# RWKV-7 mixer: one layout for both directions, halves and heads, and a recurrence without GpSimd arithmetic

## The chip, the cores and the metric

The kernel runs on one core of a Trainium2 chip. The metric is the device time of one execution in microseconds (us), the median of the runs. The engines are named as in the profile: PE is TensorE's matmul stream and PEld its loads of stationary operands, DVE is VectorE, ACT is ScalarE, POOL is GpSimd, SP is SyncE, which here only issues DMA transfers. TensorE runs at one of two clock levels, 1.2 and 2.4 GHz; the profile shows the share of the full one that was granted (PEclk).

## The reference, cut to what matters

The model is a trunk of two layers. A layer mixes tokens by three groups of heads in parallel and ends in a mixture of experts. The change is in the first group, the bidirectional RWKV-7 recurrence, and in the input columns of the two attention groups beside it. The recurrence, over 256 context and 1024 latent tokens, with 4 heads of 64 and two directions:

```
def _rwkv7_step(state, inp):                 # state: direction, head, v, k
    r, w, k, v, kk, a = inp
    sk = einsum('dbhvk,dbhk->dbhv', state, kk)
    state = state * w[..., None, :] - sk[..., :, None] * (kk * a)[..., None, :] \
            + v[..., :, None] * k[..., None, :]
    return state, einsum('dbhvk,dbhk->dbhv', state, r)
```

Here w is the decay, a the learning rate of a token, kk the normalised key, and k depends on the direction through a. The columns of the attentions are `h @ w_in`, with a rotation of q and k of the sliding-window group.

## The kernel before

The recurrence is computed in chunks of 64 tokens. A step `st` of ten handles, for both directions d, a segment of 128 tokens, that is two chunks c; heads come as two pairs hp with a head e of each pair in one half of the 128 partitions (`hom[e]`). So there are 8 units (d, hp, c) in each half.

Function `rwkv` has three parts for each step.

1. `front(st)` loads r, k, kk and the low-rank inputs, computes decays and their sums along a chunk (`cum`, by a scan, line 746) and forms scaled operands: `kd`, the direction's key (line 765, POOL), `L1` with kk and r times the decays (lines 776 and 777, DVE for e = 0 and POOL for e = 1), `bk` with the counterparts (line 784 on DVE, 785 on POOL), and `bw` (line 788, POOL). It is called for the next step ahead of the work of the present one.
2. Per step, products of `bk` and `L1` inside a chunk (line 824, tile `pa`, two banks, one for each e) are masked into `L1`, `Ly` and `low` (lines 829 to 833, 841). `low` is a lower triangle of 64 x 64 for each unit. Its inverse is made in `inv16`: the 16 x 16 blocks go through memory (`lan`) into a layout with a block on a partition, are inverted by 28 small DVE operations (lines 955 and 956) and come back through memory (`inv`); then products at line 853 (`pe`, `pzt`, `pz`), 864, 873 and 875 join the blocks.
3. Two scan steps s, one for each chunk: the old state X times `L1` (line 904, `px`), a copy (906), a product with the inverse (912), the negated values into X (913 on ACT, 914 on DVE), products for the new state and the output (924, 926), and the new state (930) from the decayed old one (`xw`, line 897, POOL). Outputs `ys` are added in eight DVE operations (935) and stored once a step by SP. New values are put in X by `new_pvu` (line 713, ACT).

Beside it, `in_BC` computes the attention columns. A column tile is 24 matmuls into one PSUM bank (lines 528 to 530, or 539 to 541), then ACT scales the result (1065), for the rotated tiles TensorE, DVE and POOL rotate it (1068 to 1072), and `part` splits it in a high and a low float16 half (1042 on ACT, 1043 on POOL). It is a generator; `more()` advances it at three places of a step.

The order of each engine's instructions is not that of the code. A scheduler takes the next instruction by a timeline that it computes when the kernel is built; the engines then run their lists in order. Rotating buffers (two PSUM banks for parts 1 and 2, two for the scan steps, one for the inverse, three for the columns) decide how far it can run ahead.

The line that splits a product's operand between engines, and the one that gives a tile two banks:

```
eng = v if e == 0 else g                                                     # before line 776
pas = [ps.tile([P, 512], F32, tag=tag, name="pa") for _ in range(2)]         # before line 824
```

## Time and profile before

| | us |
|---|---|
| median of 3 runs (lowest to highest) | 3548.71 (3547.73 to 3562.64) |
| the profiled execution | 3544.36 |
| its span | 3541.6 |
| PE busy | 2930.6 (83%) |
| DVE busy | 2285.5 (65%) |
| ACT busy | 1544.1 (44%) |
| POOL busy | 1007.7 (28%) |

Busy shares are means over stages of different kinds: the input columns of the recurrence, the recurrence with the attention columns beside it, the attentions, the output projection, the experts, for each layer. In the slices of the page below, of 88.5 us each, the recurrence fills the slices 3 to 8 of layer 0 and 23 to 28 of layer 1. DVE's digits reach 8 there, TensorE's are 8 and 9 for the most part.

### The profile page before, as it was taken

Reading aid. Unit: us, or ns where it says so; the run is one execution under the profiler, and the core shown is the slowest. Engines: PE = TensorE matmul, PEld = TensorE weight load, DVE = VectorE, ACT = ScalarE, POOL = GpSimd, SP = SyncE. Lnnn points to the kernel's source line nnn. Section 1 sums busy time; section 2 is a strip of 40 time slices with the busy share of each in tenths; the row PEclk is TensorE's granted clock in tenths of the full one; section 3 lists DMA queues with packets and bytes.
Section 4 is the critical chain, followed back from the end, with each engine's and each line's share of the span. In section 5 each row is a group of like instructions: output and inputs, shape, how many; then the busy total and the mean of one; then the engine's idle time right before and its main releaser. Section 6 shows DMA issues by size and latency. Waiting matters only on the chain. (4 is left out here: it accounts for less than half of the span.)

```text
span 3541.6 us, 71217 instructions
## 1 busy us (share of the span) xinstructions
PE 2930.6 (83%) x28620; PEld 1833.0 (52%) x28620; DVE 2285.5 (65%) x4614; ACT 1544.1 (44%) x2769; POOL 1007.7 (28%) x998
## 2 busy tenths in 40 slices
PE   7998889989998788888737998898889866778864
PEld 4656567666755444443325565666666443334431
DVE  4356877368769454557678677783776845554775
ACT  4342444345643154456544434443565314343651
POOL 1122453134424211111165225331433321101113
PEclk9998889999999899999858988899899978888987
DMA  9764343282355789999862542433732769899995
GB/s 375 297 194 111 80 104 89 70 237 71 113 176 199 278 315 384 385 379 367 334 227 78 158 106 77 105 103 95 200 107 73 258 235 363 338 393 364 349 347 198
DMA packets 425468, 773.11 MB, mean 218 GB/s; under 512 B 211152, under 2 KB 340848, under 8 KB 394160
## 3 DMA queue, kind: packets, MB, share of 16 engines
q1 hardware_dynamic: 388048, 697.84, 56.7%
q0 software_dynamic: 36368, 68.07, 5.7%
q8 instruction: 227, 3.72, 0.4%
q10 hardware_dynamic: 720, 2.62, 0.3%
q14 instruction: 105, 0.86, 0.1%
HBM read 653.31 MB, written 114.97 MB: 217 GB/s over the span
## 5 line engine op out<-in xcount | busy, mean ns | idle before, releaser
L1664 PE MATMUL pgate<-wgp,hT 128*32 128x256 f16 (+2 forms) x1704 | 353.1, 376 | 101.8 <-ACT wgp L1613 60.8
L1664 PEld LDWEIGHTS <-hT 128*32 128x32 f16 (+2 forms) x3408 | 206.7, 108 | 334.0 <-issue 172.7
L529 PE MATMUL acc<-hL,wH 128*128 128x256 f16 (+2 forms) x1040 | 346.4, 334 | 13.4 <-POOL hL L486 13.4
L528 PE MATMUL acc<-hH,wH 128*128 128x256 f16 (+2 forms) x1040 | 345.6, 335 | 7.6 <-DVE hH L485 6.6
L530 PE MATMUL acc<-hH,wL 128*128 128x256 f16 (+2 forms) x1040 | 345.4, 333 | 0.0
L1704 PE MATMUL pd<-wdp,gT 128*32 128x256 f16 (+2 forms) x1704 | 221.1, 369 | 37.6 <-DVE gT L1691 21.6
L1195 POOL TENSOR_SCALAR s<-s,rd 128x640 f32<-128x640 f32 (+2 forms) x216 | 171.6, 794 | 222.3 <-DVE rd L1191 97.4
L1622 POOL DMA_INDIRECT xg<-hmoe,map x69 | 87.7, 1271 | 508.4 <-PE ptx L1628 454.5
L1664 PE MATMUL pgate<-wup,hT 128*32 128x256 f16 (+1 forms) x1224 | 196.9, 347 | 19.8 <-DVE wup L1614 12.7
L1614 DVE SCALAR_TENSOR_TENSOR wgp<-wg,wgp 128x2048 f16<-128x2048 f32 x74 | 166.4, 2287 | 63.2 <-ACT wgp L1613 63.1
L1614 DVE SCALAR_TENSOR_TENSOR wdp<-wd,wdp 128x2048 f16<-128x2048 f32 x74 | 166.5, 2287 | 46.9 <-ACT wdp L1613 46.9
L1184 ACT ACTIVATE s<-s,nm 128x640 f32<-128x640 f32 (+2 forms) x216 | 164.4, 763 | 66.1 <-DVE nm L1181 48.6
L1614 DVE SCALAR_TENSOR_TENSOR wup<-wu,wup 128x2048 f16<-128x2048 f32 x74 | 166.3, 2286 | 30.0 <-ACT wup L1613 27.7
L1208 PE MATMUL po<-pt,vt 128*64 128x128 f32 x1920 | 166.9, 288 | 20.2 <-DVE pt L1199 11.7
L1293 PE MATMUL acco<-wo,o 128*128 128x512 f16 x756 | 177.2, 388 | 0.0
L1704 PEld LDWEIGHTS <-gT 128*32 128x32 f16 (+2 forms) x1704 | 97.0, 108 | 147.4 <-DVE gT L1691 30.0
L1613 ACT ACTIVATE wdp<-wd 128x2048 f16<-128x2048 f32 x74 | 137.2, 1903 | 51.0 <-DMA wd<-w_down 44.1
L1717 POOL DMA_DIRECT2D ys<-y x66 | 51.7, 784 | 378.5 <-DVE y L1711 206.9
L1613 ACT ACTIVATE wup<-wu 128x2048 f16<-128x2048 f32 x74 | 137.3, 1903 | 48.7 <-DMA wu<-w_up 48.7
L1613 ACT ACTIVATE wgp<-wg 128x2048 f16<-128x2048 f32 x74 | 137.4, 1902 | 46.0 <-DMA wg<-w_gate 42.7
L1165 PE MATMUL pss<-k,qs 128*128 128x256 f16 (+1 forms) x552 | 127.5, 269 | 31.9 <-DVE mx L1178 18.4
L1672 ACT ACTIVATE sg<-pgate 64x512 f32<-64x512 f32 (+2 forms) x86 | 42.8, 498 | 251.9 <-PE pgate L1664 251.9
(420 smaller groups left out, 7424.2 us busy)
## 6 DMA issues: line engine op xcount, KB each, us to landing
wu<-w_up SPq DMA_DIRECT2D x64, 2048.0 KB
wd<-w_down SPq DMA_DIRECT2D x64, 2048.0 KB
wg<-w_gate SPq DMA_DIRECT2D x64, 2048.0 KB
wmod<-w_mod SPq DMA_DIRECT2D x48, 1024.0 KB
w<-w_in SPq DMA_DIRECT2D x41, 512.0 KB
ld<-ys SPq DMA_DIRECT2D x40, 384.0 KB
z<-inv SPq DMA_DIRECT2D x80, 128.0 KB
ys<-y POOLq DMA_DIRECT2D x20, 512.0 KB
```

Source lines behind the costliest of these rows:

```text
L528: self.nc.tensor.matmul(ov, H[:, k, :], hh, start=k == 0, stop=False)
L529: self.nc.tensor.matmul(ov, H[:, k, :], hl, start=False, stop=False)
L530: self.nc.tensor.matmul(ov, Lo[:, k, :], hh, start=False, stop=k == KD - 1)
L1165: te.matmul(pss[:, o:o + n], qs[:, e, Q], k1[:, e, k0:k0 + n], start=True, stop=False)
L1184: a.activation(s2[:, e, :nk], s2[:, e, :nk], AF.Exp, bias=nm[:, e:e + 1], scale=1.0 / SS, accum_out=den[:, e:e + 1])
L1195: g.tensor_scalar(s2[:, e, :nk], s2[:, e, :nk], rd[:, e:e + 1], SC_Q, OP.mult, OP.mult)
L1208: te.matmul(po[64 * e:64 * e + 64, 0:P], vt[:, kb, 64 * e:64 * e + 64], pt[:, e, x * P:x * P + P], start=x == 0, stop=x == len(kbs) - 1)
L1293: te.matmul(acc, o[:, zo, k] if k < KD - 1 else self.og_last[:, zo, tok], wo[:, zw, k, c], start=k == 0 and y == 0, stop=k == KD - 1 and y ...
L1613: nc.scalar.mul(t[:, 0, c], w[:, c], SC_W)
L1614: nc.vector.scalar_tensor_tensor(t[:, 1, c], w[:, c], SC_W, t[:, 0, c], OP.mult, OP.subtract)
L1664: te.matmul(p[off + i * m:off + i * m + m, :n], part(hT, zh)[:, k, o:o + m], part(w, zw)[:, k, i * n:i * n + n], start=k == 0 and y == 0, ...
L1704: te.matmul(t, part(gT, zh)[:, k, :m], part(wd, zw)[:, k, i * n:i * n + n], start=k == 0 and y == 0, stop=k == 3 and y == len(parts) - 1)
```

## The change

The tiles `L1`, `L2`, `Ly`, `X`, `xy` get another order of their axes, so that one operation covers both directions or both halves, where two or four did. The product at line 824 is split: the part that goes to the other half (`pk`, one bank for both halves, line 825 of the new file) and, as products of 64 columns, those for `Ly` (`pr`, 839) and `low` (`pf`, 842, now for both directions). The products of the inverse at 853 (now 862) take only the 32 of 64 columns that are not known to be zero or unchanged; their result E lies in a tile of its own, E4, that is cleared once a layer. POOL's operations in `front`, `xw`, the rotation and the low halves go to DVE, and `bw` goes to ACT in eight pieces. Tiles that are not rotated are no longer copied before they are split: ACT writes the high half and DVE the low one, both from the accumulator. `ys` is stored for each direction and scan step, the values are loaded in three transfers in place of two.

```diff
+        E4 = rp.tile([P, 8, 64], F32, name=f"E4{l}")
+        g.memset(E4, 0.0)
...
-            for d, seg in enumerate((FSEG[st], BSEG[st])):
-                nc.sync.dma_start(vt[st][:, d], self.vst[:, 2 * seg:2 * seg + 2])
+            nc.sync.dma_start(vt[st][:, :, 0], self.vst[:, 2 * FSEG[st]:2 * FSEG[st] + 2])
+            for s in range(2):
+                nc.sync.dma_start(vt[st][:, s, 1], self.vst[:, 2 * BSEG[st] + 1 - s])
...
-            for d in range(2):
-                for e in range(2):
-                    o = hom[1 - e]
-                    a.copy(t[o, d, :, :, e, :], vt[st][o, d, s if d == 0 else 1 - s].unsqueeze(1).to_broadcast([64, 2, 2, 64]))
+            for e in range(2):
+                o = hom[1 - e]
+                a.copy(t[o, :, :, :, e, :].rearrange("p x d h v -> p x (d h) v"),
+                       vt[st][o, s].rearrange("p d h v -> p (d h) v").unsqueeze(1).to_broadcast([64, 2, 4, 64]))
...
-                for hp in range(2):
-                    v.tensor_tensor_scan(cum[:, d, hp], k2("scan"), th[:, d, hp], 0.0, OP.mult, OP.add)
+                v.tensor_tensor_scan(cum[:, d].rearrange("p h t -> p (h t)"), k2("scan"), th[:, d].rearrange("p h t -> p (h t)"), 0.0, OP.mult, OP.add)
...
-            g.tensor_tensor(kd, ta, k_, OP.mult)
+            v.tensor_tensor(kd, ta, k_, OP.mult)
...
-            for d in range(2):
-                for e in range(2):
-                    eng = v if e == 0 else g
-                    eng.tensor_tensor(L1v[hom[e], d, :, e, e], chv(kk_)[hom[e], d], chv(ex)[hom[e], d], OP.mult)
-                    eng.tensor_tensor(L1v[hom[e], d, :, e, 1 - e], chv(r_)[hom[e], d], chv(cum)[hom[e], d], OP.mult)
...
-                g.tensor_tensor(bku[o, :, 1 - e], units(kd)[o], units(wv)[o], OP.mult)
+                v.tensor_tensor(bku[o, :, 1 - e], units(kd)[o], units(wv)[o], OP.mult)
+            L1p = L1.rearrange("p d h c e s t -> p d (h c) e s t")
+            for e in range(2):
+                o = hom[e]
+                for i, (x, y) in enumerate(((kk_, ex), (r_, cum))):
+                    v.tensor_tensor(L1p[o, :, :, e, i], pieces(x)[o], pieces(y)[o], OP.mult)
...
-            g.tensor_tensor(bw.rearrange("p d h c s t -> p (d h c) (s t)"), bk.rearrange("p d h c s t -> p (d h c) (s t)"),
-                            wt.rearrange("p d h c -> p (d h c)").unsqueeze(2).to_broadcast([P, 8, 128]), OP.mult)
+            wtu = wt.rearrange("p d h c -> p (d h c)")
+            for i, (x, y) in enumerate(((bw[:, d, h, c], bk[:, d, h, c]) for d in range(2) for h in range(2) for c in range(2))):
+                a.activation(x, y, AF.Copy, scale=wtu[:, i:i + 1])
...
-                pas = [ps.tile([P, 512], F32, tag=tag, name="pa") for _ in range(2)]
+                pk = ps.tile([P, 4, 128], F32, tag=tag, name="pk")
...
-                            te.matmul(pas[e][:, i * 128:i * 128 + 128], bk[hom[e], d, hp, c].rearrange("p s t -> p (s t)"),
-                                      L1[hom[e], d, c, hp, e].rearrange("p s t -> p (s t)"), start=True, stop=True)
+                            te.matmul(pk[hom[1 - e], 2 * hp + c], bk[hom[e], d, hp, c, 1 - e, :],
+                                      L1[hom[e], d, hp, c, e].rearrange("p s t -> p (s t)"), start=True, stop=True)
...
+                            te.matmul(pr[hom[e], i], b_, r1, start=True, stop=True)
+
+                            x, y = (K_, b_) if d == 0 else (b_, K_)
+                            te.matmul(pf[hom[e], i], x, y, start=True, stop=True)
+            v.tensor_tensor(Ly.rearrange("p d h c t -> p d (h c) t"), pr.rearrange("p (d u) t -> p d u t", d=2),
+                            k2("mR").rearrange("p (d t) -> p d t", d=2).unsqueeze(2).to_broadcast([P, 2, 4, 64]), OP.mult)
+            v.tensor_tensor(low.rearrange("p d h c t -> p (d h c) t"), pf, k2("mLow").unsqueeze(1).to_broadcast([P, 8, 64]), OP.mult)
...
-            E = rp.tile([P, 8, 64], F32, tag="E", name="E", bufs=1)
-            v.tensor_tensor(E, mm8("pe4", lowu, zt16), k2("mE4").unsqueeze(1).to_broadcast([P, 8, 64]), OP.mult)
-            v.tensor_tensor(zt16, zt16, mm8("pzt", z16, E), OP.subtract)
-            v.tensor_tensor(z16, z16, mm8("pz", E, z16), OP.subtract)
+            lo16, up16 = halves(z16)[:, :, :, 0], halves(zt16)[:, :, :, 1]
+            Eh = halves(E4)[:, :, :, 1]
+            v.tensor_tensor(Eh, mm8("pe4", lowu, up16), k2("mE4").rearrange("p (g t) -> p g t", t=16).unsqueeze(1).to_broadcast([P, 8, 2, 16]), OP.mult)
+            pzt = mm8("pzt", z16, Eh)
+            v.tensor_tensor(up16, up16, pzt, OP.subtract)
+            v.tensor_tensor(lo16, lo16, mm8("pz", E4, lo16), OP.subtract)
...
-                        g.tensor_tensor(xw[hom[e]], X[hom[e], :, 0, :, e, :], w, OP.mult)
+                        v.tensor_tensor(xw[hom[e]], X[hom[e], 0, :, :, e, :], w, OP.mult)
...
-                for e in range(2):
-                    o = hom[1 - e]
-                    for d in range(2):
-                        c = s if d == 0 else 1 - s
-                        v.tensor_tensor(ys[o, d, c], pm[o, 1, d], xy[o, d, :, e, :], OP.add)
+                ys = rp.tile([P, 2, 2, 64], F32, tag="ys", name="ys", bufs=2)
+                v.tensor_tensor(ys, pm[:, 1], xy[:, 1], OP.add)
+                for d in range(2):
+                    nc.sync.dma_start(y_d[d, 2 * seg[d] + cs[d]], ys[:, d])
...
-                        nc.gpsimd.tensor_tensor(f, f, rope[:, 0, t0 - L:t0 - L + n], OP.mult)
-                        nc.gpsimd.tensor_tensor(f, f, xp, OP.add)
...
+                        nc.vector.tensor_tensor(f, f, rope[:, 0, t0 - L:t0 - L + n], OP.mult)
+                        nc.vector.tensor_tensor(f, f, xp, OP.add)
+                        nc.scalar.copy(hi, f[:, :n])
+                        nc.vector.tensor_tensor(lo, f[:, :n], hi, OP.subtract)
+                    else:
+                        nc.scalar.mul(hi, acc, down)
+                        nc.vector.scalar_tensor_tensor(lo, acc, down, hi, OP.mult, OP.subtract)
```

The first place where the order moves is VectorE's list in layer 1, around `front` for the sixth step. Here `L_23465` is the L1 of that step, `L_22942` that of the step at work, `il` and `zl` belong to the inverse. Before:

```order
L761 SCALAR_TENSOR_TENSOR th<-ta,ld 128x512
L955 TENSOR_TENSOR il<-al,zl 64x50
L776 TENSOR_TENSOR L_23465<-ld,ex 64x2x2x64 x2
L784 SCALAR_TENSOR_TENSOR bk<-th,wv 64x8x64 x2
L956 TENSOR_TENSOR zl<-zl,il 64x5x10
L829 TENSOR_TENSOR L_22942<-pa,c_20752 64x2x2x128
L831 TENSOR_TENSOR Ly<-pa,c_20752 64x2x2x64
L833 TENSOR_TENSOR low<-pa,c_20752 64x256
L777 TENSOR_TENSOR L_23465<-ld,cum 64x2x2x64 x2
L841 TENSOR_TENSOR low<-pf,c_20752 128x256
```

After, with `L_23563` and `L_23030` in their places:

```order
L764 SCALAR_TENSOR_TENSOR th<-ta,ld 128x512
L962 TENSOR_TENSOR zl<-zl,il 64x14
L784 SCALAR_TENSOR_TENSOR bk<-th,wv 64x8x64 x2
L963 COPY zl<-zl 64x256
L1077 TENSOR_TENSOR qhl<-qf,qhl 128x512
L790 TENSOR_TENSOR L_23563<-ld,ex 64x8x64
L790 TENSOR_TENSOR L_23563<-ld,cum 64x8x64
L790 TENSOR_TENSOR L_23563<-ld,ex 64x8x64
L790 TENSOR_TENSOR L_23563<-ld,cum 64x8x64
L768 TENSOR_TENSOR kd<-ta,ld 128x512
L829 TENSOR_TENSOR L_23030<-pk,c_20810 64x4x128 x4
L785 TENSOR_TENSOR bk<-kd,wv 64x8x64 x2
```

The operands of the step ahead stood in two pairs and two pairs of half width, with the inverse's steps and the masks between them; now they are ten wide operations, of which the last pair (line 785) stands behind the masks of the present step.

The second is TensorE's list in the same layer, where the products of line 824 stood in halves among the columns. Before, for the second step:

```order
L541 LDWEIGHTS hH_19273
L541 MATMUL accn<-wL,hH_19273 128x128
L824 MATMUL pa<-L_20876,bk 128x128 x4
L539 LDWEIGHTS hH_19273
L539 MATMUL accn<-wH,hH_19273 128x128
L824 MATMUL pa<-L_20876,bk 128x128 x4
L540 LDWEIGHTS hL_19274
L540 MATMUL accn<-wH,hL_19274 128x128
```

After, for the fifth step; 13 of the 20 steps have such a block of 16:

```order
L528 MATMUL acc<-hH_19331,wH 128x512
L915 MATMUL px<-pvu,L_21851 64x64 x16
L825 MATMUL pk<-L_23030,bk 64x128 x16
L529 LDWEIGHTS wH
L529 MATMUL acc<-hL_19332,wH 128x512
L530 LDWEIGHTS wL
```

A block of four is of one half, since the two halves write to different banks; the block of 16 holds both directions and alternates between the halves. The third is the masks' other products, of the ninth step of layer 1. Before (fifth step), one run of eight:

```order
L912 MATMUL pu_22815<-xy,z_1_22629 64x64 x4
L912 MATMUL pu_22815<-xy,z_0_22625 64x64 x4
L840 MATMUL pf<-bk,L_22942 64x64 x8
L529 LDWEIGHTS wH
L529 MATMUL acc<-hL_19274,wH 128x512
L530 LDWEIGHTS wL
```

After, with both products of a half one behind the other:

```order
L839 MATMUL pr<-L_25190,bk 64x64 x9
L842 MATMUL pf<-bk,L_25190 64x64 x8
L842 MATMUL pf<-L_25190,bk 64x64
L839 MATMUL pr<-L_25190,bk 64x64
L842 MATMUL pf<-L_25190,bk 64x64
L839 MATMUL pr<-L_25190,bk 64x64
```

The run of `pf` for one direction alone became runs of `pr` and `pf`, and in its later part the two alternate.

## Rows read from the trace of the kernel before

**Rows 1.** Busy time by stretch: us, then each engine's busy time (instructions), PEclk, DMA.
```profile
215.00:707.00 492.00, 435.65 (x5751) 308.61 (x5750) 331.15 (x761) 192.31 (x481) 172.70 (x171) 0.91 0.39 102
1985.00:2465.00 480.00, 434.40 (x5799) 305.31 (x5798) 332.31 (x764) 192.75 (x479) 176.56 (x164) 0.91 0.38 101
sum 972.00, PE 870.05 PEld 613.92 DVE 663.47 ACT 385.06 POOL 349.26; mean PE 435.02 PEld 306.96 DVE 331.73 ACT 192.53 POOL 174.63
```

**Rows 2.** TensorE's waits between 215 and 2465 us: us, times, longest.
```profile
PE pe L853 <- DMA z<-inv: 22.5, 15, 3.9
PE pmy L926 <- DVE pvu L914: 21.9, 7, 9.4
PE pzt L853 <- DVE E L857: 1.7, 3, 0.8
```

**Rows 3.** Busy time in two short stretches of layer 1.
```profile
2134.50:2144.00 9.50, 0.13 (x4) 0.07 (x4) 9.30 (x19) 1.91 (x3) 8.49 (x5) 0.71 0.30 83
2144.00:2149.00 5.00, 5.00 (x67) 3.46 (x68) 4.03 (x13) 2.58 (x8) 0.00 (x1) 0.52 0.47 84
```

**Rows 4.** Single lines on VectorE: duration in ns, min/median/max, over the whole run.
```profile
L777 DVE TENSOR_TENSOR L<-ld,cum x40: 404/986/1483, 243.9 to 2370.8; 64x256 f32<-64x256 f32 x40
L955 DVE TENSOR_TENSOR il<-al,zl x280: 141/196/1940, 286.2 to 2411.2; 64x14 f32<-64x14 f32 x20, 64x36 f32<-64x36 f32 x20, 64x50 f32<-64x50 f32 x20, 64x56 f32<-64x56 f32 x20
L956 DVE TENSOR_TENSOR zl<-zl,il x280: 150/196/1898, 286.4 to 2411.4; 64x14 f32<-64x14 f32 x20, 64x36 f32<-64x36 f32 x20, 64x50 f32<-64x50 f32 x20, 64x56 f32<-64x56 f32 x20
```

**Rows 5.** Groups by line on VectorE, 215 to 2465 us: busy us, mean ns | idle before.
```profile
L955 DVE TENSOR_TENSOR il<-al,zl 64x14 f32<-64x14 f32 (+6 forms) x280 | 77.2, 276 | 7.7
L956 DVE TENSOR_TENSOR zl<-zl,il 64x14 f32<-64x14 f32 (+6 forms) x280 | 71.0, 254 | 7.7
L784 DVE SCALAR_TENSOR_TENSOR bk<-th,wv 64x512 f32<-64x512 f32 x40 | 46.1, 1152 | 1.3 <-ACT wv L756 0.7
L777 DVE TENSOR_TENSOR L<-ld,cum 64x256 f32<-64x256 f32 x40 | 42.5, 1095 | 0.2
L776 DVE TENSOR_TENSOR L<-ld,ex 64x256 f32<-64x256 f32 x40 | 35.4, 918 | 0.7 <-ACT ex L757 0.5
```

**Rows 6.** Groups by line and shape on VectorE, whole run.
```profile
L829 DVE TENSOR_TENSOR L<-pa,c 64x512 f32<-64x512 f32 x80 | 54.8, 684 | 11.1 <-PE pa L824 10.2
L935 DVE TENSOR_TENSOR ys<-pmy,xy 64x128 f32<-64x128 f32 x160 | 39.0, 283 | 8.0 <-PE pmy L924 7.5
L930 DVE TENSOR_TENSOR pvu<-pmy,xw 64x256 f32<-64x256 f32 x76 | 32.0, 422 | 45.1 <-PE pmy L924 40.1 <-POOL qhl L1043 1.8 <-POOL bk L785 1.6
```

**Rows 7.** TensorE's groups by shape, whole run; line 853 alone, both stretches.
```profile
L824 PE MATMUL pa<-L,bk 64*128 64x128 f32 x640 | 80.5, 310 | 12.0 <-DVE zl L956 5.2 <-DVE Ly L831 4.2 <-ACT L L812 2.4
L840 PE MATMUL pf<-bk,L 64*64 64x64 f32 x320 | 17.0, 235 | 2.8 <-DVE low L833 2.8
L864 PE MATMUL pe<-z,low 32*32 32x32 f32 x640 | 15.8, 200 | 8.9 <-DVE z L859 8.9
...
sum 972.00, PE 84.74 PEld 71.89; mean PE 42.37 PEld 35.94
```

**Rows 8.** TensorE in order of time: start us, us, what, count.
```profile
468.83 1.16 PE L824 MATMUL pa<-L,bk 64*128 64x128 f32 x16
...
482.18 0.63 PE L840 MATMUL pf<-bk,L 64*64 64x64 f32 x16
...
2280.40 1.16 PE L824 MATMUL pa<-L,bk 64*128 64x128 f32 x8
```

**Rows 9.** ScalarE's groups by shape, whole run; SyncE's issues of line 940.
```profile
L713 ACT COPY pvu<-vt 64x256 f32<-64x256 f32 x160 | 64.3, 403 | 129.3 <-PE pmy L924 119.1 <-DVE zl L956 4.4 <-DVE il L955 4.3
L1042 ACT CAST qhl<-qf 128x512 f16<-128x512 f32 x40 | 24.7, 616 | 30.2 <-POOL qf L1072 29.5
L1054 ACT ACTIVATE vf<-accn 128x128 f32<-128x128 f32 x80 | 21.3, 276 | 56.7 <-PE accn L541 49.6 <-DMA Cv<-vf 6.0 <-POOL qhl L1043 0.8
...
L940 SPq DMA_DIRECT2D ys<-ys x40: 372/421/2721, 383.8 to 2461.9; - x40
```

More of the change, by code (lines that the diff above doesn't have):

```diff
@@ L190, in _consts @@
     for k in range(2):
[L191 to L192 removed]
+        d[f"mL1_{k}"] = np.tile(np.concatenate([sm[k], im[k]], 1), (2, 1))
+    d["mR"] = np.tile(np.concatenate(im, 1), (2, 1))
     d["mLow"] = np.concatenate([lo, lo], 0)
@@ L195, in _consts @@
     e4 = ((q[:, None] // 32 == q[None, :] // 32) & (q[:, None] % 32 < 16) & (q[None, :] % 32 >= 16)).astype(np.float32)
-    d["mE4"] = np.concatenate([e4, e4], 0)
-    d["scan"] = np.tile((np.arange(128) % 64 != 0).astype(np.float32), (128, 1))
+    d["mE4"] = np.tile(e4[:, q % 32 >= 16], (2, 1))
+    d["scan"] = np.tile((np.arange(256) % 64 != 0).astype(np.float32), (128, 1))
     d["i16"] = np.tile(np.eye(16).reshape(1, 256), (128, 1))
@@ L835, in rwkv @@
-            pf = ps.tile([P, 512], F32, tag=tag, name="pf")
-            for hp in range(2):
-                for c in range(2):
-                    for e in range(2):
-                        i = 2 * hp + c
-                        te.matmul(pf[hom[e], i * 64:i * 64 + 64], L1[hom[e], 0, c, hp, e, e, :], bk[hom[e], 0, hp, c, e, :], start=True, stop=True)
-            v.tensor_tensor(low[:, 0], pf[:, 0:256].rearrange("p (h c t) -> p h c t", h=2, c=2), mask("mLow", slice(0, 128), 64), OP.mult)
+                            te.matmul(pk[hom[1 - e], 2 * hp + c], bk[hom[e], d, hp, c, 1 - e, :],
+                                      L1[hom[e], d, hp, c, e].rearrange("p s t -> p (s t)"), start=True, stop=True)
@@ new lines, in rwkv @@
+                for e in range(2):
+                    o = hom[1 - e]
+                    v.tensor_tensor(L1[o, d, :, :, e].rearrange("p h c s t -> p (h c) (s t)"), pk[o],
+                                    k2(f"mL1_{d}")[o].unsqueeze(1).to_broadcast([64, 4, 128]), OP.mult)
+            pr = ps.tile([P, 8, 64], F32, tag=tag, name="pr")
+            pf = ps.tile([P, 8, 64], F32, tag=tag, name="pf")
+            for d in range(2):
+                for hp in range(2):
+                    for c in range(2):
+                        for e in range(2):
+                            i = 4 * d + 2 * hp + c
+                            b_, K_, r1 = bk[hom[e], d, hp, c, e, :], L1[hom[e], d, hp, c, e, 0, :], L1[hom[e], d, hp, c, e, 1, :]
+                            te.matmul(pr[hom[e], i], b_, r1, start=True, stop=True)
+                            x, y = (K_, b_) if d == 0 else (b_, K_)
+                            te.matmul(pf[hom[e], i], x, y, start=True, stop=True)
@@ L896, in rwkv @@
                         w = bass.AP(tensor=w.tensor, offset=w.offset + s, ap=[w.ap[0], [5 - 2 * s, 2], [2, 2], [0, 64]])
-                        g.tensor_tensor(xw[hom[e]], X[hom[e], :, 0, :, e, :], w, OP.mult)
+                        v.tensor_tensor(xw[hom[e]], X[hom[e], 0, :, :, e, :], w, OP.mult)
                 px = psc.tile([P, 2, 2, 2, 64], F32, tag=tagc, name="px")
-                for d in range(2):
-                    c = s if d == 0 else 1 - s
-                    for hp in range(2):
-                        for e in range(2):
-                            for sl in range(2):
-                                te.matmul(px[hom[sl], d, hp, e, :], L1[:, d, c, hp, e, sl, :], X[:, d, 0, hp, e, :], start=True, stop=True)
+                for sl in range(2):
+                    for d in range(2):
+                        for hp in range(2):
+                            for e in range(2):
+                                te.matmul(px[hom[e ^ sl], sl, d, hp, :], L1[:, d, hp, cs[d], e, sl, :], X[:, 0, d, hp, e, :], start=True, stop=True)
                 xy = rp.tile([P, 2, 2, 2, 64], F32, tag="xy", name="xy")
@@ L938, in rwkv @@
             more()
-            for d in range(2):
-                nc.sync.dma_start(y_d[d, 2 * seg[d]:2 * seg[d] + 2].rearrange("c p h t -> p c h t"), ys[:, d])
     def inv16(self, rp, b):
@@ L1038, in in_BC @@
         nc.sync.dma_start(rope, self.A["rope"])
-        def part(dst, src):
-            nc.scalar.copy(dst[:, 0], src)
-            nc.gpsimd.tensor_tensor(dst[:, 1], src, dst[:, 0], OP.subtract)
         for kind, i, _ in sorted((c for c in COL_TILES if c[0] != "A"), key=lambda c: (c[0][0], c[0] != "Bv")):
@@ L1063, in in_BC @@
                     yield
-                    f = bp.tile([P, 512], F32, tag="qf", name="qf", bufs=2)
-                    nc.scalar.mul(f[:, :n], acc, down)
+                    hl = bp.tile([P, 2, 512], F16, tag="qhl", name="qhl", bufs=2)
+                    hi, lo = hl[:, 0, :n], hl[:, 1, :n]
                     if kind[0] == "B" and t0:
+                        f = bp.tile([P, 512], F32, tag="qf", name="qf", bufs=2)
+                        nc.scalar.mul(f[:, :n], acc, down)
                         pr = ps.tile([P, 512], F32, tag=tag, name="prope")
```

54 lines of the change are left out of this document (19 added, 35 removed).

## Prediction

> **What bounds the kernel now.** I read the page's slices first, then the busy time of every engine over the two stretches in which the recurrence runs, 215 to 707 us (layer 0) and 1985 to 2465 us (layer 1). All instructions that the change touches lie in them; the order of the rest stays as it was but for small shifts. In both stretches TensorE is busy for about 90% of the time, VectorE for 68%, ScalarE for 40%, GpSimd for 36%, and the granted clock is 0.91 [rows 1]. The reader should see that no other engine comes near TensorE. It always has something to do there, since the input columns of the two attentions (line 528 and the like) are laid between the steps; a run of them still stands behind the last step in both layers. So a shorter chain of the recurrence is worth nothing by itself: only TensorE's own work, its idle time, and its clock count.
>
> Its idle time is 972.00 - 870.05 = 102 us. The list of who waited for whom names VectorE in nine rows that belong to these stretches, 63 us in all, from 21.9 us for the negated values of line 914 down to 1.7; the way of the small inverse through memory takes 22.5 us, ScalarE most of the rest [rows 2]. Next I looked at what VectorE does meanwhile. The longest gap is that of 9.4 us [rows 2]. In it VectorE works for 9.30 of 9.50 us and GpSimd for 8.49, TensorE for 0.13; in the 5 us behind it TensorE is granted 0.52 of its clock, which is the lower level of 1.2 GHz, and is busy all the time [rows 3]. That VectorE is not working normally then is seen in single lines: the 256-column product of line 777 takes 404 ns at least and 1095 in the mean, the 512-column one of line 784 has a mean of 1152, the small steps of the inverse in lines 955 and 956 have a median of 196 ns, a longest of 1940, and means of 276 and 254 [rows 4, 5]. Operations of the same widths with one operand from PSUM (829, 930) take 684 and 422 [rows 6]. The long ones read two SBUF operands while GpSimd works on such operands too.
>
> **VectorE's work, part by part.** I count 684 ns for 512 columns, 422 for 256, 283 for 128 [rows 6].
> - Contention that goes, since GpSimd has no arithmetic left there: 40 x (1095 - 404) + 40 x (918 - 404) + 40 x (1152 - 684) ns = 67 us, and 280 x (80 + 58) ns = 39 us of the inverse [rows 4 to 6]: -106 us.
> - What comes over from GpSimd: 20 + 40 operations of 512 columns (kd, the other half of bk) 41 us; line 777's kind turns from 80 of 256 into 80 of 512 columns, 80 x 0.26 = +21; 76 of 256 (xw) 32; 32 of 512 (rotation) 22; the low halves, 40 of 512 and 14 of 256, 33. Together +149.
> - What merging both directions or halves saves: Ly 80 x 0.422 - 20 x 0.684 = 20; low about 11 (60 of 256 columns against 20 of 512); the three updates of the inverse at half width 60 x 0.26 = 16; ys 160 x 0.283 - 40 x 0.422 = 28. The scans are half as many and twice as long; the trace has no 256-column scan, so it lies between 20 us saved (length fixed) and nothing; I take 0. Together -75.
> The sum is -32 us of 663, so 65% busy in place of 68% [rows 1]. Its bounds are -32 - 20 and, if nothing of the lengthening goes (each operation slow by itself), +74. VectorE gets no great relief in the mean. What it loses is operations that take two or three times their length at the wrong moment.
>
> **TensorE's work.** The product of line 824 took 80.5 us for 640 instructions, 126 ns each [rows 7]. Sixteen that alternate between the two partition halves take 1.16 us, eight of one half take the same 1.16 us [rows 8], so halves overlap when they alternate, and the old order often split them. The new pk writes both halves into one bank, and the order shows 16 in a row. At 1.16 / 16 that is 46 us, at a clock like today's 51: -30 (bounds -34 and 0). The products for Ly and low, apart now, are 1280 instructions in place of 320 at 53 ns [rows 7]: +51. Where pr and pf of one half follow each other they can't overlap; so the bounds are 1280 x 39 ns (a block of 16 took 0.63 us [rows 8]), +33, and double that, +84. The three products of the inverse are 1920 instructions in 84.7 us, 44 ns each; at 32 columns line 864's 15.8 / 640 = 25 ns apply [rows 7]: -37 (bounds -37 and 0). Net -16, from -38 to +84.
> The Trainium skill has a rule against the last part: in "TensorEngine Tiling (Array Packing)", section Instruction Overhead, a matmul with very few columns takes as long as one of about 60. By it the -37 would be 0. The rows differ: 32 columns cost 25 ns where 64 cost 44, so I keep -37, and put the rule among the rivals.
>
> **TensorE's idle time.** Of the 63 us behind VectorE I take 60%, -38. Bounds: all 63, and 0. Not all goes, since the block ahead of a step is as long as before: one operation of line 761's kind, kd, four bk and four L1, ten of 684 ns = 6.8 us, against 0.68 + 2 x 1.152 + 2 x 0.918 + 2 x 1.095 = 7.0 us [rows 5, 6]. What goes is the stretching of the inverse behind it, and the wait of bk's second half and bw for GpSimd's queue. The 22.5 us behind memory stay. New behind VectorE: xw, queued between the new state and the next products, and the reads of the accumulators for the low halves.
>
> **The clock.** A granted mean of 0.91 over 972 us loses 87 us of full-rate work [rows 1]. Low clock follows gaps, as in [rows 3]. With 38 of 102 us of idle time gone, 37% of the loss would go too, 32 us; I count two thirds, -22, since some of it lies where TensorE would wait anyway. Bounds 0 and -50.
>
> **ScalarE and the queues.** bw moves there as 160 copies of 128 columns, nearest row 276 ns, +44 us [rows 9] (bounds: the 196 ns of VectorE's small steps and the 403 of a wider copy, +31 and +64). Off go: half of the value copies, the rest twice as wide (160 x 403 against 80 x 616 ns, -15), and the second pass over 38 accumulators (24 x 616 ns and 14 of half the width, -19) [rows 9]. Its sum is +10 of 385 [rows 1], in parts of 0.28 us. But bw is a block of eight, 2.2 us, and copies of the recurrence queue behind it; half of one in a quarter of the 20 steps is +6. SP issues three more transfers a step (two of ys, one of the values): 60 x 0.42 = 25 us on its queue [rows 9], with bounds 0 and +10 on the path because the inverse's loads queue there too; I take 0. The cleared E4 and the two memsets are outside the loop.
>
> **Sum.** -16 - 38 - 22 + 6 = -70 us on the profiled execution's 3544.4 us (2.8 us around the span), 3474. The median of the runs is 4.3 us above that execution: 3479.
>
> **Rivals.**
> 1. The waits are passed on. In place of VectorE the trip through memory or ScalarE's block of bw is late; idle time and clock stay, and only the products change: -16 + 6 = -10, 3539. For it: 22.5 us behind memory already [rows 2]. Against: this trip starts from low, which VectorE writes, and its 28 steps are those that were stretched.
> 2. Slower. VectorE now frees the accumulators of 38 column tiles, which ScalarE freed alone; a read behind the block of 6.8 us holds its bank, and with three banks TensorE's filler stops. It decides from the point where VectorE is so late that both other banks are full. 38 x 6.8 = 258 us if nothing hid it; a fifth exposed is +52, the idle and clock gains gone: -10 + 52 = +42, 3591. For it: every gap behind VectorE now can hit the filler too. Against: 65% busy [rows 1], and the tiles are spread over ten steps a layer.
> 3. Half-width products save nothing: the forecast without its -37, -33, 3516. That is the rule named above, worked out from [rows 7]; these rows speak against it.
> 4. The clock comes back almost wholly: idle -63, clock -50, products -16: with +6 it is -123, 3426. For it: low clock follows gaps only, and the gaps thin out.
>
> **How the numbers follow.** Forecast 0.63 (own range 3440 to 3515), rival 1 0.14, 2 0.07, 3 0.06, 4 0.10. A measurement tells about 0.5% (18 us) from no change. Faster: forecast, 3, 4 and a fifth of rival 1, 0.82. Same: the rest of rival 1, 0.11. Slower: rival 2, 0.07. The range takes in rival 4 and rival 1 almost to no change: 3430 to 3545.
>
> **What would show it.** Right: 256- and 512-column operations of VectorE within a few per cent of 420 and 685 ns and no means above medians in the inverse; VectorE's rows in TensorE's waits at about 25 us; the granted clock near 0.94; pk below 55 us, pr and pf near 70 together, the inverse's three near 47; the two stretches 35 us shorter each. Wrong: a gap list as long as now under other names, waits of the column products (528, 539) for VectorE, or a pr-pf cost near 100 us. The prediction fails as a whole if the clock stays at 0.91.

## The result and the profile after

The changed kernel takes 3511.52 us (median; 3509.44 to 3523.29). Its ratio to the kernel before is 0.9904, 95% interval 0.9880 to 0.9928: about 34 us less by the ratio, 37 by the medians. The forecast was 3479, 70 us less: the direction was right, the size twice too large.

The two stretches first, here from the recurrence's first product to the last column product. In the kernel before they take 1000.9 us, TensorE is busy for 896.0 and idle for 104.6:

```profile
215.70:734.40 518.70, 459.70 (x6038) 327.11 (x6037) 338.01 (x781) 198.39 (x497) 179.04 (x178) 0.91 0.42 111
1985.00:2467.20 482.20, 436.33 (x5830) 307.07 (x5828) 332.31 (x764) 193.25 (x481) 176.56 (x164) 0.91 0.38 101
sum 1000.90, PE 896.03 PEld 634.17 DVE 670.33 ACT 391.64 POOL 355.60; mean PE 448.02 PEld 317.09 DVE 335.16 ACT 195.82 POOL 177.80
```

After:

```profile
216.40:731.40 515.00, 457.52 (x6517) 329.07 (x6517) 315.96 (x766) 203.37 (x495) 4.14 (x14) 0.91 0.44 115
1974.90:2438.60 463.70, 425.40 (x6317) 301.62 (x6315) 304.81 (x742) 198.21 (x485) 0.82 (x5) 0.93 0.41 105
sum 978.70, PE 882.92 PEld 630.69 DVE 620.77 ACT 401.58 POOL 4.96; mean PE 441.46 PEld 315.35 DVE 310.39 ACT 200.79 POOL 2.48
```

Columns as in [rows 1]. Idle time here and below is the sum of TensorE's gaps from the first product to the last; the windows, rounded outwards, hold a few tenths of a us more. The stretches are 22 us shorter, not 70: busy time fell by 13 us, idle time by 9 only (to 95.5), and the clock is where it was in layer 0. The other 12 us lie outside the stretches, in stages that the change doesn't touch. Single executions of the kernels below (e4 aside) differ there from the kernel before by -26 to +8 us, once the wait ahead of the attention (see the table) is counted to the stretch, and I give these no cause.

VectorE's groups by line in the changed kernel (busy us, mean ns | idle before):

```profile
L962 DVE TENSOR_TENSOR zl<-zl,il 64x14 f32<-64x14 f32 (+6 forms) x280 | 53.5, 191 | 7.4
L961 DVE TENSOR_TENSOR il<-al,zl 64x14 f32<-64x14 f32 (+6 forms) x280 | 53.4, 191 | 7.6
L784 DVE SCALAR_TENSOR_TENSOR bk<-th,wv 64x512 f32<-64x512 f32 x40 | 27.4, 686 | 1.2
L790 DVE TENSOR_TENSOR L<-ld,cum 64x512 f32<-64x512 f32 x40 | 27.3, 684 | 0.3
```

Against [rows 5] the lengthening beside GpSimd ("stretching" below) is gone: the inverse's steps take 191 ns where they took 276 and 254, line 784 takes 686 where it took 1152. This is what was forecast. Yet TensorE's waits (us, times, longest) are these:

```profile
PE pe L862 <- DMA z<-inv: 33.5, 20, 4.7
PE pe L875 <- DVE z L870: 17.3, 7, 5.3
PE pmy L935 <- DVE pvu L924: 13.0, 10, 4.2
PE pu L922 <- ACT xy L917: 7.5, 6, 2.2
```

The wait for pvu fell from 21.9 [rows 2] to 13.0 us, that for the inverse's trip through memory rose from 22.5 to 33.5 and stands in all 20 steps, and the join of line 875 waits 17.3 us, where its counterpart, line 864, waited 8.9 [rows 7]. All rows behind VectorE together fell from 63 to 42 us, where the prediction looked for 25.

The trip itself didn't get longer. From SyncE's first store of a step's blocks (`lan`) to the end of its last load (`z`) it took 26.9 us before and 26.2 after (medians of the 20 steps). TensorE has less else to do meanwhile, as the last column of the table below will show. TensorE's groups by shape, where [rows 7] had 80.5, 17.0 and, for line 853, 84.74 us:

```profile
L839 PE MATMUL pr<-L,bk 64*64 64x64 f32 x640 | 45.0, 240 | 4.0 <-DVE L L829 4.0
L825 PE MATMUL pk<-L,bk 64*64 64x128 f32 x640 | 43.3, 275 | 0.9 <-ACT L L817 0.9
L862 PE MATMUL pe<-z,low 64*64 64x32 f32 x640 | 34.2, 245 | 33.8 <-DMA z<-inv 33.5
L842 PE MATMUL pf<-L,bk 64*64 64x64 f32 x320 | 26.3, 241 | 0.0
L862 PE MATMUL pzt<-E,z 64*64 64x32 f32 x640 | 25.0, 227 | 0.0
L862 PE MATMUL pz<-z,E 64*64 64x32 f32 x640 | 24.4, 226 | 2.6 <-DVE z L869 2.6
L842 PE MATMUL pf<-bk,L 64*64 64x64 f32 x320 | 20.5, 246 | 1.9 <-DVE L L829 1.0 <-DVE zl L962 0.8
```

The reader should see that the inverse's three products (line 862), half as wide now, take 83.6 us: as much as before. The rows of pr and pf overlap in time, so they can't be added up. What all products that read `bk` occupy together (lines 824 and 840 before; pk, pr and pf after) is this, before and after:

```profile
sum 1000.90, PE 97.43; mean PE 48.71
sum 978.70, PE 104.97; mean PE 52.48
```

### The profile page after: what moved, and what is told of

Same layout as the page of the kernel before. It is cut to its first block, busy times and chain, and to the rows that moved or that the text cites. A ratio compares the mean times of both kernels' runs of the same rounds, so it can differ in the third digit from the quotient of the medians.

```text
span 3507.8 us, 72584 instructions
## 1 busy us (share of the span) xinstructions
PE 2919.4 (83%) x29580; PEld 1827.5 (52%) x29580; DVE 2224.4 (63%) x4576; ACT 1553.7 (44%) x2771; POOL 649.8 (19%) x678
## 5 line engine op out<-in xcount | busy, mean ns | idle before, releaser
L1620 DVE SCALAR_TENSOR_TENSOR wup<-wu,wup 128x2048 f16<-128x2048 f32 x74 | 166.2, 2286 | 27.0 <-ACT wup L1619 26.9
L530 PEld LDWEIGHTS <-wL 128*128 128x128 f16 (+1 forms) x1040 | 105.6, 102 | 87.6 <-issue 28.7
```

The lines of the kernel that those rows point to most:

```text
L530: self.nc.tensor.matmul(ov, Lo[:, k, :], hh, start=False, stop=k == KD - 1)
L1620: nc.vector.scalar_tensor_tensor(t[:, 1, c], w[:, c], SC_W, t[:, 0, c], OP.mult, OP.subtract)
```

## Experiments

All ratios are to the kernel before, run on the same chip. "Columns" is read from TensorE's list, not from a duration: the column products that stand between the inverse's groups (pe4, pzt, pz, pe5, p5), summed over the 20 steps at 66, 110 and 215 ns for 128, 256 and 512 moved columns. In the changed kernel's trace they follow each other every 56, 109 and 216 ns (medians). The sum says how much work TensorE is given while that chain runs. "To attention" is the idle time if the stretch is taken on to the attention's first product. The difference is 12 to 14 us in most kernels, and 25 to 41 us in e7, e8, e9 and e11. There at most 11 us of columns are left behind the last step of layer 0, where the others have 30 or more, and TensorE waits for the attention's k out of memory. So these four gained less idle time than the column "idle" says.

| kernel | ratio (95%) | stretches us | busy | idle | to attention | clock | columns us |
|---|---|---|---|---|---|---|---|
| before | 1 | 1000.9 | 896.0 | 104.6 | 117.8 | .91 .91 | 151 |
| changed | 0.9904 (0.9880-0.9928) | 978.7 | 882.9 | 95.5 | 108.8 | .91 .93 | 117 |
| e2 full width | 0.9797 (0.9772-0.9822) | 937.6 | 864.8 | 72.5 | 84.8 | .95 .95 | 144 |
| e3 GpSimd back | 1.0138 (1.0111-1.0165) | 1057.9 | 905.0 | 152.6 | 165.0 | .87 .90 | 96 |
| e5 changed, reversed | 0.9861 (0.9838-0.9884) | 968.6 | 868.7 | 99.5 | 112.7 | .92 .94 | 117 |
| e6 full width, reversed | 0.9773 (0.9754-0.9793) | 927.6 | 856.6 | 70.7 | 83.7 | .96 .96 | 144 |
| e7 move only | 0.9742 (0.9721-0.9762) | 899.3 | 864.5 | 34.5 | 68.6 | .98 .96 | 181 |
| e8 joint products | 0.9697 (0.9679-0.9714) | 900.8 | 862.3 | 37.9 | 62.7 | .97 .98 | 173 |
| e9 joint, half width | 0.9780 (0.9757-0.9803) | 925.7 | 880.3 | 44.8 | 71.4 | .96 .94 | 156 |
| e10 alternating | 0.9880 (0.9857-0.9903) | 974.4 | 871.7 | 102.3 | 116.0 | .92 .93 | 101 |
| e11 joint, two banks | 0.9779 (0.9758-0.9800) | 915.6 | 837.9 | 77.4 | 118.0 | .97 .94 | 168 |
| e12 half width, full list | 0.9785 (0.9758-0.9812) | 939.1 | 866.6 | 72.2 | 84.6 | .94 .95 | 144 |

**e1, what a small product costs.**

```diff
+            seq("mA", 48, 64, 64, 64)    # products, rows, stationary, moved columns
+            seq("mB", 48, 64, 64, 32)
+            seq("mC", 48, 64, 32, 32)
...
```

> The changed kernel with an added block of float32 products on constants in its setup (nothing left out): 24 wide ones to start with, then rows of 48 that alternate between the two partition halves, by stationary x moved columns: A 64x64, B 64x32, C 32x32 on 64 rows, D 32x64, E 32x32 on 32 rows, F 64x128, G 128x128 in two banks, H 64x64 with two of the same half in a row, I 64x16. Theory 1 (a product of the inverse is paced by its stationary operand, not by its moved columns): A and B within 10% of each other, about 40 ns each, C clearly less, about 25 ns as line 864 was; I as B. Rival (columns pace it): A about 40, B and C both about 25 ns, D like A. For the other products: F 55 to 73 ns, G 73, H between 40 and 79 (79 if two of one half do not overlap at all).

TensorE in order of time (start us, us, what, count):

```profile
26.30 3.01 PE L405 MATMUL mA<-msrc 64*64 64x64 f32 x96
29.39 2.99 PE L405 MATMUL mB<-msrc 64*64 64x32 f32 x96
32.44 1.71 PE L405 MATMUL mC<-msrc 64*32 64x32 f32 x96
...
35.26 2.70 PE L405 MATMUL mD<-msrc 64*32 64x64 f32 x89 [0.63 <-issue]
...
41.51 7.12 PE L405 MATMUL mF<-msrc 64*64 64x128 f32 x96
48.70 5.63 PE L405 MATMUL mG<-msrc 64*128 64x128 f32 x96
54.38 3.06 PE L405 MATMUL mH<-msrc 64*64 64x64 f32 x96
57.50 2.98 PE L405 MATMUL mI<-msrc 64*64 64x16 f32 x96
```

A record is half a product. With 64 stationary columns a record takes 31 ns whether 64, 32 or 16 columns are moved (A, B, I); with 32 stationary ones 18 for 32 moved (C) and 30 for 64 (D). So the larger of the two sets the pace in these rows, and theory 1 holds, with times a quarter below those it named. G, 128 by 128, takes 59. F, 64 by 128, took 7.12 us, with the clock at 0.76 in it; in its later part, where the clock was full, its pairs of records came 109 ns apart, 55 each, hardly less than G. H, pairs of one half, takes 32, as much as alternating halves (A) and less than the expected 40 to 79. E, 32 by 32 on 32 rows, ran in two parts with a gap of 1.53 us between them, about 20 each.

**e2, full width again.**

```diff
-            pzt = mm8("pzt", z16, Eh)
+            pzt = halves(mm8("pzt", z16, E4))[:, :, :, 1]
...                                                            # pe4 and pz likewise
```

> The changed kernel with the inverse's three products of 64 moved columns again, VectorE's updates left at half width. Theory 1 (half-width products saved nothing): these products stay at 84 us within 4, and the time stays within 12 us of the changed kernel, 0.987 to 0.994 of the kernel before. Rival (they did save, and something else ate it): the products come to 105 to 120 us and the time is 20 to 37 us longer, 0.996 to 1.001 of before.

The products took 87.18 us where the half-wide ones took 83.58 (line 862 alone, by stretch), as theory 1 had it. Both expectations of the time missed: it is shorter, by 1.1% of the kernel before. The width changed next to nothing in the products and 23 us in idle time, with the clock 0.02 to 0.04 higher. Its waits:

```profile
PE pe L862 <- DMA z<-inv: 24.6, 16, 3.2
PE pmy L935 <- DVE pvu L924: 12.0, 7, 5.4
PE pe L875 <- DVE z L870: 5.1, 4, 2.0
```

Those behind the inverse fell by 21 us, from 33.5 and 17.3: nearly all of the 23. What the expectations below call theory 3 comes from here: the scheduler takes a wider product to last longer and puts more columns beside it. The list agrees: 144 us of columns in place of 117.

**e3, GpSimd's arithmetic back, the rest kept.**

```diff
-            v.tensor_tensor(kd, ta, k_, OP.mult)
+            g.tensor_tensor(kd, ta, k_, OP.mult)
...                                                   # bk, L1 (e = 1), bw, xw, rotation, low halves likewise
```

> The changed kernel with the layouts kept and the arithmetic of the recurrence, of the rotation and of the low halves back on GpSimd (kd, the second half of bk, one half of L1, bw, xw). Theory A (what the change won came from GpSimd leaving VectorE's operands): VectorE's operations on two SBUF operands stretch again (means 30% or more above medians in the inverse), TensorE waits some 55 to 65 us for VectorE in the two stretches, and the time is 0.996 to 1.004 of the kernel before. Theory B (merging and the products won it, and the stretching was hidden): 0.985 to 0.993.

Theory A, and more than it asked: slower than the kernel before, by 1.4%. VectorE, and the longest wait behind it:

```profile
L960 DVE TENSOR_TENSOR il<-al,zl 64x14 f32<-64x14 f32 (+6 forms) x280 | 84.9, 303 | 7.7
L790 DVE TENSOR_TENSOR L<-ld,cum 64x512 f32<-64x512 f32 x20 | 33.2, 1658 | 0.5 <-ACT cum L761 0.5
```

```profile
PE pmy L934 <- DVE pvu L923: 39.5, 12, 8.1
```

**e4, no wait for the trip.**

```diff
-                nc.sync.dma_start(z[64 * e:64 * e + 64], self.unit_rows(self.inv[b][j], e))
+                nc.sync.dma_start(z[64 * e:64 * e + 64], self.unit_rows(self.invz, e))
```

> The changed kernel, but the 16x16 block inverses that the joining products read come from a cleared buffer, not from the one that the inverse writes (the inverse is still computed and stored; its result is left out of the joins). So TensorE cannot wait for that trip. Theory 1 (idle time is passed on along the chain of a step, so that taking one wait away gives back less than it): of the 33.5 us that TensorE waited for the trip at most half is won, 0.983 to 0.990 of the kernel before. Rival (each wait counts by itself): idle time falls by 30 us or more and with the clock the time by 35 to 50 us, 0.976 to 0.981 of before.

The kernel leaves the blocks' inverses out of the joins, which read a cleared buffer. The whole time (ratio 1.0704) says nothing: other values send other rows to the experts. The stretches do:

```profile
215.50:676.70 461.20, 437.38 (x6524) 313.76 (x6523) 313.12 (x766) 204.97 (x495) 3.50 (x14) 0.96 0.50 130
2055.80:2498.30 442.50, 410.34 (x6310) 290.05 (x6308) 307.72 (x751) 198.43 (x486) 4.24 (x10) 0.97 0.44 115
```

903.7 us, 75 less than the changed kernel's: idle 55.7, 40 less, and the clock at 0.96. Theory 1, that waits are mostly passed on, falls, and the gain is larger than the rival's too. But it is not the price of the trip alone: without that dependence the list was laid anew as well, with 163 us of columns between the inverse's groups in place of 117, and the wait for pvu fell from 13.0 to 2.4 us.

**e5 and e6, the controls.**

```diff
-                for u in range(8):
+                for u in range(7, -1, -1):
```

> The changed kernel with the eight units of the inverse's products taken in the other order (same work, same half width): a control of how far the time moves when only the order of the lists is shuffled. Theory 3 (the width given to the products moves the time because the scheduler lays the columns by it, and not by chance): within 12 us of the changed kernel, 0.987 to 0.994 of the kernel before. Rival (chance of the order): anywhere in 0.975 to 1.000, and the next run, the same control at full width, overlaps with it.

> The kernel with full-width products of the inverse and the eight units in the other order. Theory 3: within 12 us of the full-width kernel, 0.976 to 0.983 of the kernel before, and below the half-width control. Rival (chance): 0.975 to 1.000.

The controls stay apart, 0.9861 (just below theory 3's range) and 0.9773. But the list puts the same columns at the same places as without the reversal, so they are repeats and no test of chance. As repeats they tell that one list's ratio moves by 0.2 to 0.4% between chips and sessions. Differences of this size between kernels that didn't run side by side say nothing; e5 to e8 ran on one chip.

**e7, the move alone, in the old layout.** The edit is the opposite of e3's, in the kernel before, with `bw` in eight pieces on ScalarE.

> The kernel before with its layouts, products and stores, but GpSimd's arithmetic of the recurrence, the rotation and the low halves on VectorE, bw on ScalarE in eight pieces. Theory A (GpSimd leaving the operands is what pays): VectorE's operations lose their stretching, and the time is 0.975 to 0.986 of the kernel before, less than the changed kernel needs. Rival (without the merged operations VectorE has too much to do): VectorE at 72% or more of the two stretches, TensorE's waits for it no shorter than before, 0.992 to 1.003.

Theory A: faster than the changed kernel by 1.6%, and than its control on the same chip (e5) by 1.2%.

```profile
215.10:673.20 458.10, 441.65 (x6031) 311.75 (x6029) 345.36 (x915) 220.00 (x576) 0.63 (x10) 0.98 0.42 112
1942.70:2383.90 441.20, 422.80 (x5825) 296.77 (x5824) 341.95 (x908) 215.13 (x561) 1.15 (x7) 0.96 0.41 109
```

VectorE is busy for 76% here, more than in any other version, and TensorE is idle for 34.5 us only in the stretches. The trip costs 5.0 us of waiting, although it takes longer than in the other kernels named above: 33.2 us from the first store to the last load. The list has 181 us of columns beside the chain. But few of them are left at the end, and TensorE waits for the attention's operands:

```profile
PE pss L1166 <- DMA k<-Bk: 34.1, 2, 19.0
```

In the changed kernel this wait is 13.3 us. Counted with it, the move took 49 us of idle time, not 70.

**e8, joint products.**

```diff
-                pk = ps.tile([P, 4, 128], F32, tag=tag, name="pk")
+                pas = [ps.tile([P, 4, 2, 64], F32, tag=tag, name="pa") for _ in range(2)]
...
+                for i in range(4):
+                    for e in range(2):
+                        te.matmul(pas[e][:, i].rearrange("p s t -> p (s t)"), bk[hom[e], d, i // 2, i % 2].rearrange("p s t -> p (s t)"),
+                                  L1[hom[e], d, i // 2, i % 2, e].rearrange("p s t -> p (s t)"), start=True, stop=True)
...
```

> The full-width kernel of the second run, with the products for the masks joined again as in the kernel before (128 stationary by 128 moved columns into two banks, line 824's kind, and 64-column products for low of one direction), in the new layout; of the masks those of one kind stand together, so that the two banks come free close to each other. By the rows of 128x128 and of 64x128 in the first run (59 and 74 ns) the joined product costs no more than the short one. Theory 1: TensorE's work for the masks falls from 92 us to 55 to 65 us, VectorE gets 31 us more, and the time is 0.966 to 0.975 of the kernel before. Rival (the order splits the halves again, as it did before): 80 us or more for these products and 0.978 to 0.988.

The time is as theory 1 had it, 0.9697, the best of all: 3444 us against 3547. The reason isn't, or in small part only:

```profile
L824 PE MATMUL pa<-L,bk 64*128 64x128 f32 x640 | 74.1, 289 | 2.1 <-DVE Ly L833 1.9 <-ACT L L817 0.2
L837 PE MATMUL pf<-bk,L 64*64 64x64 f32 x320 | 15.2, 225 | 0.0
```

89 us, above the rival's bound of 80: the list still splits the halves. All products that read `bk` occupy 103.9 us in e2 and 89.1 here, 15 less. But TensorE's busy time as a whole is 862 us as in e2 (865). Idle time fell from 72.5 to 37.9 (to the attention, from 84.8 to 62.7), with 173 us of columns in place of 144.

**e9, joint products and half width.** The edit is e2's, taken back.

> The joint-products kernel of the run before, with the inverse's products at half width again. In TensorE's list the columns that stand between the inverse's four groups of products (pe4 to p5, 20 steps) come to 117 us of column work in the changed kernel, 144 with full width, 181 with the move alone, 173 with joint products, and in their traces TensorE was idle for 95, 73, 35 and 38 us in the two stretches. Here the list has 156. Theory 3 (idle time is what the list has too little between them): idle 53 to 65 us, and 0.974 to 0.981 of the kernel before. Rival (half width costs only together with split products): idle 35 to 45, 0.966 to 0.972.

0.9780 is in theory 3's range and outside the rival's: half width costs 0.8% here too, if e8's value from another chip may stand beside it. Idle time, 44.8, is in the rival's range and not in theory 3's 53 to 65; most of the loss shows in busy time (880.3 against 862.3) at a clock of 0.95 in place of 0.975. Nor does TensorE wait more behind the inverse, as it did in e2's case. The trip's wait is half of e8's 17.0 us, and the longest one is another:

```profile
PE px L908 <- DVE pvu L932: 9.9, 7, 2.8
PE pe L855 <- DMA z<-inv: 8.2, 7, 2.0
```

So why half width costs time with joint products is open.

**e10, all pr, then all pf.** The loop with both products of a unit becomes two loops.

> The changed kernel, with all products pr emitted before all products pf, so that each row alternates between the halves. The list has 101 us of columns between the inverse's groups, 16 less than the changed kernel. Theory 3: idle 105 to 118 us in the two stretches, 0.991 to 0.999 of the kernel before. Rival (pairs of one half cost TensorE time, and the new order spares it): 5 to 15 us less for pr and pf, 0.980 to 0.988. The row H of the first run speaks against the rival: pairs of one half took no longer than alternating ones.

Neither: 0.9880 lies between the two values of the changed list (0.9904 and e5's 0.9861), and idle time, 102.3, is 3 us short of the forecast. 16 us fewer columns in the list cost less than theory 3 says, and not where it says: the waits behind the inverse fell from 51 to 21 us, those for pvu rose from 15 to 42. pr and pf fell from 91.8 to 67.1 us by their rows, but all products that read `bk` occupy 102.8 us, against 105.0 and 103.4 in the two runs of the changed list: rows of products that interleave count time twice. Pairs of one half cost TensorE next to nothing, as in row H.

**e11, two banks as one tile.**

```diff
+        e_psr, psr = opened("psRw", bufs=1, space=PSUM, side="right")    # for the recurrence
...
+                pas = ps.tile([P, 2, 4, 2, 64], F32, tag=tag, name="pa")    # pu, pb and pf likewise
...
```

> The joint-products kernel with the two banks of a pair taken as one tile (one buffer of two banks for everything that took two of one), so that the halves can always alternate. In the list 168 us of columns stand between the inverse's groups, against 173. The joint products alternate in part only now (56 ns where they do, 112 where not, 109 in the mean with what surrounds them). Theory: they fall from 70 to 45 to 55 us, idle time is 38 to 50 us, 0.960 to 0.969 of the kernel before. Rival (a pair that comes free together comes free later, and the step's chain waits for it): idle 55 us or more, 0.971 to 0.985.

Time and idle time are the rival's. The joint products fell to 59.3 us and TensorE's busy time to 837.9, the least of all; idle time doubled to 77.4 (to the attention 118.0, as in the kernel before), although the list had 168 us of columns. How late a bank comes free is not in that count. That this is the cause is argued, not shown: the largest wait in the stretches is again the trip's, 30.7 us against 17.0 in e8.

**e12, the changed products in the full-width list.**

```diff
...
+                aps = []
+                for p in (x.ins[0], x.outs[0]):
...
+                    aps.append(copy.replace(p, ap=[[512, 64], [32, 2], [1, 16]], offset=p.offset + cut[x.name], bass_ap=None))
+                new[n] = copy.replace(x, ins=[aps[0], x.ins[1]], outs=[aps[1]])
...
```

> The full-width kernel of the second run, scheduled with the inverse's products at 64 moved columns, and only then, with every engine's list fixed, these 960 products cut to the 32 columns that the changed kernel moves. So the chip gets the products of the changed kernel in the lists of the full-width one. Theory 3 (what the width changes is the list, by what the scheduler takes a product to cost): the time of the full-width kernel, 0.976 to 0.983 of the kernel before, idle time 65 to 80 us in the two stretches. Rival (half-width products are slow or disturb something on the chip, for instance by their operands in pieces of 16): the time of the changed kernel, 0.986 to 0.992, idle time above 90 us.

```profile
L864 PE MATMUL pe<-z,low 64*64 64x32 f32 x640 | 36.6, 244 | 26.2 <-DMA z<-inv 26.1
L864 PE MATMUL pz<-z,E 64*64 64x32 f32 x640 | 24.7, 221 | 1.8 <-DVE z L872 1.6
L864 PE MATMUL pzt<-E,z 64*64 64x32 f32 x640 | 24.2, 225 | 0.1
```

The products are 32 wide as in the changed kernel, and TensorE's order in the trace is that of e2 in over 99% of its records. Time (0.9785) and idle (72.2) are those of the full-width kernel. So it is shown: the half-wide products are harmless on the chip, and the list that is laid for them costs about 1% (0.9904 and 0.9861 against 0.9797, 0.9773 and 0.9785).

## Why the prediction was wrong

In the profiled execution the change gave -13 us of TensorE's busy time, -9 of its idle time and -12 outside the stretches. The forecast had -38 for the first (products -16, clock -22), -38 for the second, and +6 for ScalarE. Two of its steps failed: the price of the inverse's products, and the share of idle time that goes, with the clock that hangs on it. Under the second lies its first premise, "the order of the rest stays as it was but for small shifts".

By e7 and e3 the parts nearly add up: the move alone gives 0.9742, the rest 1.0138 (both without the direct split of the unrotated tiles), and their product, 0.9876, lies between the two values of the whole, 0.9904 and 0.9861. On one chip the rest divides so: new layouts with joint products 0.9742 to 0.9697 (e7, e8), split products 0.9697 to 0.9773 (e6), half width 0.9773 to 0.9861 (e5). The forecast had the move at -54 us (idle, clock, ScalarE), where it gave 2.6%, 92 us; and the products at -16, where splitting and halving cost 0.8 to 1% each.

- **VectorE's work: right.** 620.8 us busy in the stretches, from 670.3: -50, forecast -32 with bounds to -52. The -106 of contention went, as the means above show.
- **TensorE's products: wrong in the inverse.** "At 32 columns line 864's 15.8 / 640 = 25 ns apply": the -37 became -1 (84.7 to 83.6). Line 864's product is short in both operands, and I put its price down to the moved one alone; e1 separates them. B and I cost as much as A with fewer moved columns, and C, with 32 stationary ones, costs little more than half: what held was the stationary operand's 64 columns. The Trainium skill's rule ("TensorEngine Tiling (Array Packing)", Instruction Overhead), that a matmul with few moved columns takes as long as one of about 60, gave the right sum here, nothing saved. pa to pk was right (-37 by rows, forecast -30). All products that read `bk` together rose by 8 us, forecast +21; that pairs of one half can't overlap, the reason for its upper bound, H and e10 contradict. So the products came to about +6, forecast -16. Why TensorE's busy time fell by 13 all the same is not shown here.
- **Idle time and clock: right in cause, wrong for this kernel.** "Of the 63 us behind VectorE I take 60%, -38": those waits fell by 21 us, the trip's rose by 11, and idle time fell by 9 in all. The clock rose by 0.01, not 0.03; in layer 0 it stayed at 0.91, the prediction's own sign of failing. The move alone takes 70 us of idle time out of the stretches (49 with the wait ahead of the attention) and lifts the clock to 0.97, near what rival 4 said. The step left out that the scheduler lays the columns anew for every change, by what it takes each operation to cost. Half width took 27 us of columns out of the inverse's chain, and TensorE waited there instead: e2 and e12 show it. With joint products half width costs as much (e9), but not by that wait. Why the split products' list leaves 29 us fewer than the joint one was not tried apart from the products. Their `bk` products occupy 11 to 15 us more (e6, e2); that the list makes most of the 1% is argued from the equal busy times of e2 and e8.
- **ScalarE: right in load.** `bw` is 49.0 us busy (forecast +44). One piece takes 389 ns in place of 276, but the pieces of a block overlap, so that one costs 306. No wait of TensorE on it is in the list of waits. SyncE's extra issues show in no wait either, and the trip that shares its queue is no longer than before.
- **Rivals.** The first was half right: idle time and clock nearly stayed and the trip's wait rose, but the trip is not later, and the waits are not passed on by any law (e7). The second didn't come: none of TensorE's waits names the low halves. The third, 3516 us, is within 5 us of the measured time, and that is luck: it had the price of the half-wide products right, but it kept -38 of idle time and -22 for the clock, which didn't come, and put nothing for the 12 us outside the stretches.

## What to carry to other kernels

Where a scheduler lays filler (here the column products) by expected costs, an edit that makes an operation look shorter than it runs can take cover away from the chain it stands in; compare the work in the list beside the chain, not only the operation. Such a count is a help and no law: here it went with the idle time of most kernels, but not of e9 and e11. Filler that is spent early is missing at the end. Before halving an operand, look which of the two operands sets the pace. And try the parts of a change alone: here one part was worth 2.6%, and two others gave back nearly 2%.

## What the runs showed of the hardware that was not expected

GpSimd's arithmetic, 356 us busy in the two stretches, went to VectorE and ScalarE in e7 and raised their busy time by 17 us (670.3 to 687.3) and 43 us (391.6 to 435.1) only: by these sums most of what GpSimd had taken off VectorE it had cost it in stretching. And what a gap costs shows behind it: in the changed kernel one of 4.45 us (columns as in [rows 1]) is followed by 4.65 us at the lower level, 0.50 or 1.2 GHz, with TensorE busy throughout, and by a stretch at 0.58:

```profile
2158.00:2164.90 6.90, 6.90 (x95) 4.47 (x93) 6.80 (x16) 4.64 (x9) 0.00 (x0) 1.00 0.17 33
2164.90:2169.35 4.45, 0.01 (x2) 0.00 (x0) 4.33 (x7) 1.02 (x3) 0.00 (x0) 0.75 0.58 121
2169.35:2174.00 4.65, 4.64 (x76) 4.46 (x78) 4.14 (x7) 2.44 (x8) 0.00 (x0) 0.50 1.03 291
2174.00:2178.00 4.00, 4.00 (x32) 2.31 (x31) 1.76 (x3) 0.00 (x0) 0.00 (x0) 0.58 0.42 136
```
